# Half-array matmuls issued in turn over two PSUM banks in a two-block transformer kernel

## Chip, cores and metric

The kernel runs on one core of one Trainium2 chip. The metric is the device time of one execution in microseconds (us). Engines: PE (TensorE, matrix products), DVE (VectorE), ACT (ScalarE), POOL (GpSimd) and SP (SyncE, which issues most transfers). PE writes its products to PSUM, eight banks of [128, 512] floats.

## What is computed

256 tokens of width 2048 go through two blocks, each of two layers. The first block is attention: in layer 0 a sparse attention with compressed, selected and window branches, a differential attention with heads of 64 channels, and an attention over a memory; in layer 1 an attention to the 64 keys that an index score picks, and the memory again. The second block has in each layer four mixers beside each other (retention, hgrn2, mlstm, rwkv7, each 512 wide with heads of 64 channels) and a feed-forward part. The pieces with heads of 64 channels, cut from the reference:

```python
# differential attention: two score maps per head, 64 channels each
p = masked_softmax(jnp.einsum('bthcd,bshcd->bhcts', qb, k) * dq ** -0.5, key_pos[None, :] <= t[:, None])
a = p[:, :, 0] - lam * p[:, :, 1]
# index score of layer 1: 16 heads of 64 channels
rel = jax.nn.relu(jnp.einsum('bthd,bsd->bths', qi, k_idx))
score = jnp.einsum('bths,bth->bts', rel, wi)
# second block: each layer
mixed = jnp.concatenate([o_ret, o_hgrn, o_ml, o_rw], axis=-1) @ w_out[l]
h = h + rms_norm_2(mixed, norm_post_mix[l])
ffn = (jax.nn.silu(u @ w_ffn_gate[l]) * (u @ w_ffn_up[l])) @ w_ffn_down[l]
# rwkv7, per token and head of 64 channels
state = state * exp(logw) - (state kk) (a kk)^T + v k^T ;  y = state r
```

## The kernel before

All tokens stay on the chip; weights stream in pieces of [128, 1024] floats, which ACT (L205) and DVE (L206) split into two parts. Each product of a projection is three matmuls at L211 (`mm3`), which read and write the whole 128 by 128 array. In fp32, as in the mixers and attentions, one matmul of the program is two pairs of a weight load and a matmul in the trace, so a record count there is twice the program's count.

A *half-array* matmul uses 64 of the 128 rows (a product over the 64 channels of a head, operands in partitions 0 to 63 or 64 to 127) or 64 of the 128 columns (its result goes to 64 of the 128 partitions). The heads of even number lie in one half, those of odd number in the other. The sites, by the lines of the profile:

- differential attention, L451 in `soft`: per half (`c`) a bank with a mask product (L450, bf16) and a score per head in turn, then softmax on DVE and ACT. Other attentions call `soft` too, with scores over the full array.
- `pick`, L949: index scores; four (first token block) or two heads of one half per bank, then ACT's relu (L952) and one DVE instruction per head (L959).
- retention L1043 and L1044, mlstm L1235 and L1236: per head a bank, one score of 256 columns and one of 128, then DVE (mlstm L1237), then products over the full array. In mlstm the decays (L1228, L1230, exponential at L1233) of a head go first into a bank of their own.
- hgrn L1140: eight levels, per half a bank with two scores of 128 columns; L1144 (DVE) multiplies each bank with a mask. L1149 puts the results into 64 rows of bank 7 per half.
- rwkv: L1331 (low-rank inputs), L1409 and L1410 (`grams`: per source and half a bank with four products of 128 columns), L1446 and L1472 (products with the state S, in the second token block only, each followed by products over the full array into the same bank), L1481 and L1482 (update of S).

The helper `bank` takes the numbers of a use in turn; in the mixing phase rwkv has banks 3 and 4, the other mixers 5 and 6, results gathered over heads bank 7, projections 0 to 2. The final order on each engine isn't that of the code: a list scheduler of the build orders the instructions by their dependences, tiles and banks, and fills the gaps of a mixer with L211 of other projections. PE takes its instructions in that order.

Of the kernel before, what the change touches and what calls it, by code (L numbers as in the profile page):

```python
# [18 lines left out]
P = 128  # L19
T = 256  # L20
# [5 lines left out]
# ---------------------------------------------------------------- constants  # L26
# [11 lines left out]
class Slab:  # L38
    """Arrays of [128, n] packed side by side; at[name] is (offset, columns)."""
# [70 lines left out]
# ------------------------------------------------------------------ emitter  # L110
# tiles of each tag: of the whole run, of the first block, of the second block
# [4 lines left out]
# PSUM banks of each use: m projections, t their inputs' transposes, e what takes them on, x scores and transposes,  # L116
# o results gathered over heads, r rwkv
# [5 lines left out]
class Later:  # L123
    """Items that are computed where they are first asked for."""
# [10 lines left out]
def halves(x):  # L135
    """The two token blocks of a tile [128, 2, 512]."""
    return [x[:, m] for m in range(2)]


class Emitter:  # L140
# [34 lines left out]
    def on_the_way(self):  # L175
        """For what takes a projection out of PSUM, beside the attention of earlier ones."""
# [7 lines left out]
    def phase(self, **banks):  # L184
        """The numbers of the PSUM banks that each use takes in turn."""
# [12 lines left out]
    # -- weights: loaded in pieces of [128, j, n], split into two float32r parts  # L198
# [14 lines left out]
    def by_tokens(self, xg, w, c0, n):  # L213
        """x @ w[:, c0:c0+n] as two tiles [128 tokens, n]."""
# [12 lines left out]
    def by_channels(self, xg, w, c0, n):  # L227
        """(x @ w[:, c0:c0+n]).T as tiles [128 channels, 2, 256 tokens]."""
# [14 lines left out]
    def by_channels1(self, xg, w, c0, n):  # L243
        """(x @ w[:, c0:c0+n]).T, n < 128, as one tile [n, 256 tokens]."""
# [9 lines left out]
    def turned_back(self, xg, w, c0, n):  # L254
        """x @ w[:, c0:c0+n], n < 128, as two tiles [128 tokens, n]."""
# [7 lines left out]
    def group_block(self, yg, w, k0, cb):  # L263
        """y[:, k0:k0+512] @ w[k0:k0+512, cb*512:(cb+1)*512] per token block."""
# [9 lines left out]
    def out_group(self, yg, w, k0, dst, first):  # L274
        """dst[g][m] += y[:, k0:k0+512] @ w[k0:k0+512]."""
# [8 lines left out]
    # -- float32r pairs  # L284
# [3 lines left out]
    def split(self, dst, src, scale=None):  # L288
        """dst (hi, lo) = src * scale, hi rounded, lo the rest; src in PSUM or SBUF."""
# [9 lines left out]
    def transposes(self, out, srcs):  # L299
        """out[:, i] = srcs[i].T for blocks srcs[i]; out in PSUM."""  # L300
# [39 lines left out]
    def x_part(self, xg, kt, rows=slice(None)):  # L340
        """Rows of the kt-th channel block of a group list of pairs; the next group is made ahead."""
# [5 lines left out]
    def row_scale_of(self, X):  # L347
        """row_scale of X, computed when it is first needed."""
# [11 lines left out]
    def rsqrt(self, out, v, tmp, by=None):  # L360
        """out = by * v ** -0.5: a first guess from the exponent, three Newton steps; v becomes -v / 2."""
# [26 lines left out]
    def spread_rows(self, r):  # L388
        """[128, 256] with r[t] in every partition; r: [128 tokens, 2]."""
# [10 lines left out]
    def head_scale(self, src, nh, dh, rows=None, m=0, n=P, eps=EPS):  # L400
        """Per row and head r * rsqrt(mean((r * src)**2) + eps); src [n, nh*dh] in PSUM."""
# [9 lines left out]
    def gain_tables(self, tag, gain, cos, sin, dh, into=None):  # L411
        """cos * gain and sin * (gain with halves swapped), for rope of (x * gain)."""
# [1347 lines left out]
```

## Time and profile before

| | us |
|---|---|
| three timed runs: median (lowest, highest) | 3990.16 (3976.85, 3991.68) |
| span of the profiled execution | 3999.7 |
| PE busy | 3919.7 (98%) |
| DVE busy | 2377.9 (59%) |
| ACT busy | 1817.2 (45%) |
| mean granted TensorE clock | 0.972 |

The span runs from the first to the last instruction of the one profiled execution; the profile gives no other time of it, and its span lies 9.5 us above the median of the timed runs. The busy time of PE counts overlapping records once, and the end of a matmul record is modelled, so what a matmul costs is read from the start of one record to the start of the next.

### The profile page before, as it was taken

The numbers are of one execution on the slowest core, as the hardware profiler recorded it, in microseconds if no ns is written. First come the engines' busy times: TensorE is split into PE (matmuls) and PEld (weight loads), VectorE is DVE, ScalarE is ACT, GpSimd is POOL, SyncE is SP. The second block draws the span as 40 slices with busy tenths as digits, with TensorE's granted clock in tenths as the row PEclk, the third lists the DMA queues.
The fourth block names the chain that finished last, engine by engine and source line by source line (L and its number), as shares of the span: only waits on it lengthen the run. The fifth ranks groups of instructions, "written<-read, shape, count | busy, mean of one in ns | idle before, by whom it ended". The sixth has DMA issues, their size and how long they took to land.

```text
span 3999.7 us, 54714 instructions
## 1 busy us (share of the span) xinstructions
PE 3919.7 (98%) x21408; PEld 3282.1 (82%) x21408; DVE 2377.9 (59%) x4126; ACT 1817.2 (45%) x2463; POOL 0.2 (0%) x4
## 2 busy tenths in 40 slices
PE   9999999999999999999999999999999999999998
PEld 7878777788898988978888888898988978888886
DVE  6666667666664556574555556664566564555556
ACT  5545455454444355354344444534454354444443
POOL 0000000000000000000000000000000000000000
PEclk9999999999997899999999999996999999999999
DMA  7664545555632244556666666521344566666665
GB/s 237 194 174 121 168 135 146 169 168 163 196 92 59 85 127 140 171 180 184 189 185 185 185 188 187 156 81 54 94 142 143 169 190 185 185 188 184 185 187 165
DMA packets 402644, 633.64 MB, mean 158 GB/s; under 512 B 28081, under 2 KB 164017, under 8 KB 402385
## 3 DMA queue, kind: packets, MB, share of 16 engines
q1 hardware_dynamic: 399744, 624.70, 52.1%
q10 hardware_dynamic: 2640, 5.44, 0.4%
q8 instruction: 168, 2.75, 0.3%
q14 instruction: 92, 0.75, 0.1%
HBM read 623.77 MB, written 6.29 MB: 158 GB/s over the span
## 4 chain that ended last, share of the span: by engine, by line
PE 88%; DVE 6%; DMA 3%; ACT 2%; issue 1%; SPq 0%; ACTq 0%; DVEq 0%
PE b L211 73%; PE b L303 3%; DVE wlo L206 2%; PE b L1432 1%; PE b L1427 1%; PE b L451 1%; PE b L1149 1%; ACT whi L205 1%; PE b L478 1%; PE b L1140 1%; DMA wraw<-in_even_w_in_dram 0%; PE b L1409 0%; DMA wraw<-in_nsa_cmp_w_dram 0%; DMA wraw<-in_w_ffn_down_dram 0%; PE b L1230 0%
## 5 line engine op out<-in xcount | busy, mean ns | idle before, releaser
L206 DVE TENSOR_TENSOR wlo<-wraw,whi 128x1024 fp32r<-128x1024 f32 x1144 | 1393.7, 1219 | 1136.4 <-ACT whi L205 1134.4
L205 ACT CAST whi<-wraw 128x1024 fp32r<-128x1024 f32 x1144 | 1196.1, 1046 | 1567.6 <-PE b L211 1441.0
L211 PE MATMUL b<-whi,xt 128*128 128x512 f32 (+1 forms) x5888 | 1698.7, 371 | 0.0
L211 PEld LDWEIGHTS b<-whi,xt 128*128 128x128 f32 x5888 | 1062.8, 190 | 197.1 <-issue 3.7
L211 PE MATMUL b<-wlo,xt 128*128 128x512 f32 (+1 forms) x2944 | 1088.8, 370 | 3.5 <-DVE wlo L206 3.4
L211 PE MATMUL b<-whi,yt 128*128 128x512 f32 x2304 | 746.1, 400 | 1.5 <-ACT yt L293 1.5
L211 PEld LDWEIGHTS b<-wlo,xt 128*128 128x128 f32 x2944 | 559.8, 190 | 100.8 <-DVE wlo L206 7.3
L211 PE MATMUL b<-xt,whi 128*128 128x256 f32 (+3 forms) x2688 | 520.7, 291 | 2.3 <-ACT xt L296 2.0
L211 PEld LDWEIGHTS b<-whi,yt 128*128 128x128 f32 x2304 | 433.9, 189 | 108.2 <-issue 2.7
L211 PE MATMUL b<-wlo,yt 128*128 128x512 f32 x1152 | 461.8, 401 | 0.0
L211 PEld LDWEIGHTS b<-xt,whi 128*128 128x128 f32 (+3 forms) x2688 | 423.1, 191 | 14.3 <-ACT xt L296 3.3
L211 PE MATMUL b<-xt,wlo 128*128 128x256 f32 (+3 forms) x1344 | 388.9, 289 | 0.0
L211 PEld LDWEIGHTS b<-wlo,yt 128*128 128x128 f32 x1152 | 217.5, 189 | 52.4 <-issue 2.1
L211 PEld LDWEIGHTS b<-xt,wlo 128*128 128x128 f32 (+3 forms) x1344 | 256.6, 191 | 3.5 <-issue 1.5
L211 PE MATMUL b<-whi,g 128*128 128x512 f32 (+1 forms) x384 | 108.0, 360 | 0.4 <-ACT g L293 0.4
L282 DVE TENSOR_TENSOR r<-b,r 128x512 f32<-128x512 f32 x144 | 92.3, 683 | 0.0
L211 PEld LDWEIGHTS b<-whi,g 128*128 128x128 f32 (+1 forms) x384 | 61.7, 162 | 14.3 <-ACT g L293 0.9
L303 PE MATMUL b<-gains,X 128*128 128x128 f32 x232 | 39.0, 305 | 33.1 <-DVE small L370 15.6
L211 PE MATMUL b<-wlo,g 128*128 128x512 f32 (+1 forms) x192 | 68.7, 358 | 0.3 <-DVE wlo L206 0.2
L282 DVE TENSOR_TENSOR X<-b,X 128x512 f32<-128x512 f32 x96 | 63.0, 684 | 8.9 <-PE b L211 8.7
L1437 ACT COPY r<-b 128x512 f32<-128x512 f32 x40 | 23.4, 584 | 92.3 <-PE b L303 92.2
L303 PEld LDWEIGHTS b<-gains,X 128*128 128x128 f32 x232 | 30.5, 157 | 39.8 <-issue 25.9
(481 smaller groups left out, 3036.8 us busy)
## 6 DMA issues: line engine op xcount, KB each, us to landing
wraw<-in_w_in_dram SPq DMA_DIRECT2D x248, 512.0 KB, 3.7
wraw<-in_w_ffn_gate_dram SPq DMA_DIRECT2D x176, 512.0 KB, 3.7
wraw<-in_w_ffn_up_dram SPq DMA_DIRECT2D x176, 512.0 KB, 3.7
wraw<-in_w_ffn_down_dram SPq DMA_DIRECT2D x176, 512.0 KB, 3.7
wraw<-in_w_out_dram SPq DMA_DIRECT2D x128, 512.0 KB, 3.7
wraw<-in_even_w_in_dram SPq DMA_DIRECT2D x104, 512.0 KB, 3.6
wraw<-in_odd_w_in_dram SPq DMA_DIRECT2D x96, 512.0 KB, 3.6
wraw<-in_mem_w_kv_dram SPq DMA_DIRECT2D x32, 512.0 KB, 4.1
```

The lines of the kernel that those rows point to most:

```text
L205: nc.scalar.copy(hi, raw)
L206: nc.vector.tensor_sub(lo, raw, hi.bitcast(FT))
L211: self.nc.tensor.matmul(out, l[x], r[y], start=start and i == 0, stop=stop and i == 2, **kw)
L282: self.nc.vector.tensor_add(dst[cb][m], ps[m], dst[cb][m])
L303: self.nc.tensor.transpose(o, s, self.c("ident")[:n, :n])
L451: nc.tensor.matmul(ps[:, o : o + nk], l, r, start=not masks, stop=True, skip_group_check=True)
L478: self.nc.tensor.matmul(out, tt[:, i, j], vs[j], start=j == 0, stop=j == k - 1)
L1140: nc.tensor.matmul(ps[:, i], ek[r, i], eq[r, i], start=True, stop=True)
L1149: nc.tensor.matmul(out, vc[:, i * P + 64 * par : i * P + 64 * par + 64], am[:, par, i], start=False, stop=h == 1, skip_group_check=True)
L1427: mm(ps[:, i].rearrange("p (b k) -> p b k", k=h), gb[0][:, i], left(inv[:, i]), start=True, stop=True)
L1432: mm(ps[:, i], it[:, i], pl[:, i], start=True, stop=True)
L1437: nc.scalar.copy(it, b)
```

## The change

Where the halves were written one after the other, they are now written in turn: first of one half, first of the other, second of the one, and so on, into two banks that are both taken ahead. `soft` becomes `scores` (all masks first, then the scores of all sets in turn) and `exps`. In mlstm the decays of two heads come before the scores of both, and the sums for the denominator move from the decays' bank to the scores'. In rwkv the products with S of all heads come before the products that add to them. The state's update takes heads 0, 2, 1, 3. No arithmetic is added or removed. Comment lines, which the change also drops, are left out.

```diff
+    def scores(self, sets, nk):
+        nc = self.nc
+        res = [self.bank()[:, : len(items) * nk] for items in sets]
+        for ps, items in zip(res, sets):
+            for i, (_, _, masks) in enumerate(items):
+                for x, (ml, mr, mc) in enumerate(masks):
+                    o = i * nk + mc
+                    nc.tensor.matmul(ps[:, o : o + mr.shape[1]], ml, mr, start=x == 0 and i == 0, stop=False,
+                                     skip_group_check=True)
+        for i in range(len(sets[0])):
+            for ps, items in zip(res, sets):
+                l, r, masks = items[i]
+                nc.tensor.matmul(ps[:, i * nk : i * nk + nk], l, r, start=not masks and i == 0, stop=True,
+                                 skip_group_check=True)
+        return res
...
+    def pair_scores(self, qT, kT, i):
+        res = [self.bank() for _ in range(2)]
+        for ss, ts, c in ((slice(0, P), slice(0, T), slice(0, T)), (slice(P, T), slice(P, T), slice(T, 384))):
+            for par in range(2):
+                r = slice(64 * par, 64 * par + 64)
+                self.nc.tensor.matmul(res[par][:, c], kT[r, i, ss], qT[r, i, ts], start=True, stop=True)
+        return res
...
@@ hgrn
+            for i in range(2):
+                for par in range(2):
+                    r = slice(64 * par, 64 * par + 64)
+                    nc.tensor.matmul(pss[par][:, i], ek[r, i], eq[r, i], start=True, stop=True)
             for par in range(2):
-                r = slice(64 * par, 64 * par + 64)
-                ps = self.bank()[:, :T].rearrange("p (a t) -> p a t", a=2)
-                for i in range(2):
-                    nc.tensor.matmul(ps[:, i], ek[r, i], eq[r, i], start=True, stop=True)
...
@@ mlstm
+        for h in range(4):
+            if h % 2 == 0:
+                dms = [decays(h + x) for x in range(2)]
+                pss = self.pair_scores(qT, kT, h // 2)
+            dm, ps = dms[h % 2], pss[h % 2]
             nc.vector.scalar_tensor_tensor(dm, ps[:, :384], 0.125, dm, OP.mult, OP.mult)
...
-            db = pd[:, 384:386]
+            db = ps[:, 384:386]
...
@@ rwkv_half, grams
+                pss = [self.bank().rearrange("p (a x t) -> p a x t", a=2, x=2) for _ in range(2)]
+                for i in range(2):
+                    for x, by in enumerate((kk, r)):
+                        for par in range(2):
+                            q = heads[2 * par + i][2]
+                            mm(pss[par][:, i, x], src[q, i, t], by[q, i, t], start=True, stop=True)
...
@@ rwkv_half, products with the state
+            def of_state(src):
+
+                res = [self.bank()[:, :P].rearrange("p (i c) -> p i c", i=2) for _ in range(2)]
+                if S is not None:
+                    for i in range(2):
+                        for par in range(2):
+                            q = heads[2 * par + i][2]
+                            mm(res[par][:, i], src[q, i, t], S[q, i], start=i == 0, stop=False, skip_group_check=True)
+                return res
...
-                for h in range(4):
+                for h in (0, 2, 1, 3):
```

What the change does to the instructions' order, at three places of the first mixing phase. Names: `L211` is a projection's matmul, `b3` to `b7` are banks with the number of the tile behind them, `x2` means two program matmuls in a row.

PE, mlstm, around the scores of the second head before (L1235, L1236; decays at L1228, L1230):

```order
L1235 MATMUL b6_11858<-g2_11440,g2_11573 128x256
L1236 MATMUL b6_11858<-g2_11440,g2_11573 128x128
L211 MATMUL b0_11940<-xt_9177,whi_11942 128x256
L303 MATMUL b3_10819<-gains_63,r2_10815 128x128 x4
L1228 LDWEIGHTS identb2_9137
L1228 MATMUL b5_11851<-laterb_9139,identb2_9137 128x128
L1228 LDWEIGHTS identb2_9137
L1228 MATMUL b5_11851<-laterb_9139,identb2_9137 128x128
L1230 MATMUL b5_11851<-mx_11305,gains_63 128x384
```

and now around the scores of the second pair of heads (L1077 is `pair_scores`, L1251 and L1253 are the decays, L1457 and L1462 belong to rwkv):

```order
L1251 LDWEIGHTS identb2_9137
L1251 MATMUL b6_11876<-laterb_9139,identb2_9137 128x128
L1251 LDWEIGHTS identb2_9137
L1251 MATMUL b6_11876<-laterb_9139,identb2_9137 128x128
L1253 MATMUL b6_11876<-mx_11305,gains_63 128x384
L1462 MATMUL b4_10851<-r1_10849,r2_10815 128x64 x4
L1077 MATMUL b5_11883<-g2_11440,g2_11573 128x256
L1077 MATMUL b6_11884<-g2_11440,g2_11573 128x256
L303 MATMUL b3_10857<-gains_63,r2_10816 128x128 x4
L1457 MATMUL b4_10863<-r2_10816,r2_10783 128x64 x4
L1077 MATMUL b5_11883<-g2_11440,g2_11573 128x128
L1077 MATMUL b6_11884<-g2_11440,g2_11573 128x128
```

The scores of a head stood alone ahead of the next head's decays; now the decays of a second head stand ahead of both heads' scores, which alternate between banks 5 and 6.

PE, rwkv, first of the `grams`, before:

```order
L1409 MATMUL b3_10018<-r2_9692,r2_9690 128x128
L1410 MATMUL b3_10018<-r2_9688,r2_9690 128x128
L1409 MATMUL b3_10018<-r2_9692,r2_9690 128x128
L1410 MATMUL b3_10018<-r2_9688,r2_9690 128x128
L1409 MATMUL b4_10025<-r2_9692,r2_9690 128x128
L1410 MATMUL b4_10025<-r2_9688,r2_9690 128x128
L1409 MATMUL b4_10025<-r2_9692,r2_9690 128x128
L1410 MATMUL b4_10025<-r2_9688,r2_9690 128x128
```

and now:

```order
L1438 MATMUL b3_10018<-r2_9692,r2_9690 128x128
L1438 MATMUL b3_10018<-r2_9688,r2_9690 128x128
L1438 MATMUL b3_10018<-r2_9692,r2_9690 128x128
L1438 MATMUL b3_10018<-r2_9688,r2_9690 128x128
L1438 MATMUL b4_10019<-r2_9692,r2_9690 128x128
L1438 MATMUL b4_10019<-r2_9688,r2_9690 128x128
L1438 MATMUL b4_10019<-r2_9692,r2_9690 128x128
L1438 MATMUL b4_10019<-r2_9688,r2_9690 128x128
```

The code alternates, but the scheduler still sets all four products of one bank ahead of the four of the other, here and in all 16 of these sets.

PE, rwkv, second token block, products with the state (L1446, now L1476) and those that add to them (L1447, now L1486), before:

```order
L1446 MATMUL b4_10379<-st_10204,r2_9692 128x64
L1447 MATMUL b4_10379<-r2_10002,r2_10257 128x64
L1446 MATMUL b4_10379<-st_10204,r2_9692 128x64
L1447 MATMUL b4_10379<-r2_10002,r2_10257 128x64
L211 MATMUL b0_11450<-xt_9297,wlo_11543 128x256
L211 MATMUL b0_11450<-xt_9297,whi_11542 128x256
L1446 MATMUL b3_10385<-st_10204,r2_9692 128x64
L1447 MATMUL b3_10385<-r2_10002,r2_10257 128x64
L1446 MATMUL b3_10385<-st_10204,r2_9692 128x64
L1447 MATMUL b3_10385<-r2_10002,r2_10257 128x64
```

and now:

```order
L1476 MATMUL b4_10379<-st_10204,r2_9692 128x64 x2
L1486 MATMUL b4_10379<-r2_10002,r2_10257 128x64 x2
L211 MATMUL b0_11450<-xt_9297,wlo_11543 128x256
L211 MATMUL b0_11450<-xt_9297,whi_11542 128x256
L1476 MATMUL b3_10380<-st_10204,r2_9692 128x64 x2
L1486 MATMUL b3_10380<-r2_10002,r2_10257 128x64 x2
```

The two halves still stand apart, with two L211 between; within a half the two products with S now stand together. In the other places: hgrn's scores alternate in all 32 levels, its L1149 (now L1173) stood as four in a row or as two, two transposes (L303), two, and now as one, one transpose, three; retention's order stands as it was; `pick` alternates, with two to four L211 between its sets.

## Rows read from the trace of the kernel before

**Rows 1.** The page: busy time of the engines, chain of waits by engine

```profile
PE 3919.7 (98%) x21408; PEld 3282.1 (82%) x21408; DVE 2377.9 (59%) x4126; ACT 1817.2 (45%) x2463; POOL 0.2 (0%) x4
...
PE 88%; DVE 6%; DMA 3%; ACT 2%; issue 1%; SPq 0%; ACTq 0%; DVEq 0%
```

**Rows 2.** Windows, length, busy PE PEld DVE ACT POOL (instructions), granted clock, DMA share, GB/s

```profile
1080.00:1760.00 680.00, 660.00 (x4600) 590.58 (x4600) 394.96 (x784) 302.62 (x440) 0.00 (x0) 0.93 0.41 122
495.40:502.20 6.80, 6.80 (x19) 5.05 (x19) 1.61 (x7) 3.04 (x9) 0.00 (x0) 0.50 0.26 80
669.00:684.00 15.00, 14.11 (x83) 10.15 (x82) 14.19 (x40) 8.55 (x14) 0.00 (x0) 1.00 0.24 70
```

**Rows 3.** Timeline of PE (start, us, instruction, records xcount): scores of hgrn

```profile
1467.02 0.72 PE L1140 MATMUL b<-g 64*128 64x128 f32 x8
1467.67 0.50 PE L211 MATMUL b<-wlo,yt 128*128 128x512 f32 x1
```

**Rows 4.** Timeline of PE: one half of `grams` alone

```profile
1164.97 0.49 PE L1409 MATMUL b<-r,r 64*128 64x128 f32 x2
...
1166.06 0.39 PE L211 MATMUL b<-xt,whi 128*128 128x256 f32 x1
```

**Rows 5.** Timeline of PE: both halves of `grams`, four products and four

```profile
1125.89 0.49 PE L1409 MATMUL b<-r,r 64*128 64x128 f32 x2
...
1127.72 0.38 PE L211 MATMUL b<-xt,whi 128*128 128x256 f32 x1
```

**Rows 6.** Timeline of PE: retention, scores of two heads in turn

```profile
1632.20 0.71 PE L1043 MATMUL b<-g,g 64*128 64x256 f32 x4
...
1633.06 0.39 PE L211 MATMUL b<-whi,xt 128*128 128x256 f32 x1
```

**Rows 7.** Timeline of PE: products with the state, one half

```profile
1360.79 0.43 PE L1446 MATMUL b<-st,X 64*128 64x64 f32 x2
...
1361.88 0.43 PE L1447 MATMUL b<-r,r 128*128 128x64 f32 x2
1362.12 0.36 PE L211 MATMUL b<-wlo,xt 128*128 128x256 f32 x1
```

**Rows 8.** Timeline of PE: mlstm, a whole head, a divided one

```profile
1389.36 0.70 PE L1235 MATMUL b<-g,g 64*128 64x256 f32 x2
...
1390.20 0.39 PE L211 MATMUL b<-xt,whi 128*128 128x256 f32 x1
...
1392.46 0.70 PE L1235 MATMUL b<-g,g 64*128 64x256 f32 x2
1393.09 0.28 PE L1228 MATMUL b<-laterb,identb 128*128 128x128 bf16 x2
...
1394.14 0.48 PE L1236 MATMUL b<-g,g 64*128 64x128 f32 x2
1394.56 0.39 PE L211 MATMUL b<-xt,whi 128*128 128x256 f32 x1
```

**Rows 9.** Timeline of PE: differential attention, first token block, masks and scores

```profile
491.91 0.23 PE L450 MATMUL b<-futureb,identb 128*128 128x128 bf16 x1
...
497.26 0.79 PE L211 MATMUL b<-whi,xt 128*128 128x512 f32 x1
```

**Rows 10.** Timeline of PE: results of hgrn, two in a row and four

```profile
1463.19 0.65 PE L1149 MATMUL b<-g,a 128*64 128x128 f32 x4
...
1463.77 0.44 PE L303 MATMUL b<-gains,a 128*128 128x128 f32 x2
...
1469.03 0.83 PE L1149 MATMUL b<-g,a 128*64 128x128 f32 x8
1469.80 0.44 PE L303 MATMUL b<-gains,a 128*128 128x128 f32 x2
```

**Rows 11.** Groups by line (busy us, mean ns, idle before, releaser): mlstm, split weights

```profile
L206 DVE TENSOR_TENSOR wlo<-wraw,whi 128x1024 fp32r<-128x1024 f32 x1136 | 1390.2, 1224 | 1128.5 <-ACT whi L205 1126.5 <-issue 0.5
...
L1237 DVE SCALAR_TENSOR_TENSOR a<-b,a 128x384 f32<-128x384 f32 x16 | 8.9, 555 | 14.0 <-ACT a L1233 10.5 <-PE b L1236 3.5
```

More of the change, by code (lines that the diff above doesn't have):

```diff
@@ L440, in soft, with exps @@
     def soft(self, items, nk, fs):
+        return self.exps(self.scores([items], nk)[0], nk, fs)
+    def scores(self, sets, nk):
         nc = self.nc
-        n = len(items)
-        ps = self.bank()[:, : n * nk]
-        for i, (l, r, masks) in enumerate(items):
-            o = i * nk
-            for x, (ml, mr, mc) in enumerate(masks):
-                w = mr.shape[1]
-                nc.tensor.matmul(ps[:, o + mc : o + mc + w], ml, mr, start=x == 0, stop=False, skip_group_check=True)
-            nc.tensor.matmul(ps[:, o : o + nk], l, r, start=not masks, stop=True, skip_group_check=True)
+        res = [self.bank()[:, : len(items) * nk] for items in sets]
[11 more added lines that the diff above has]
+        return res
+    def exps(self, ps, nk, fs):
+        nc = self.nc
+        n = ps.shape[1] // nk
         ps3 = ps.rearrange("p (h k) -> p h k", h=n)
@@ L830, in diff @@
                 pts, cfs = [], []
+                both = (slice(0, 64), slice(64, 128))
+                scores = self.scores([[(qT[r, h, t], kT[r, h, :nk], self.causal(m)) for h in range(h0, h0 + step)]
+                                      for r in both], nk)
                 for c in range(2):
-                    r = slice(c * 64, c * 64 + 64)
-                    pt, sm = self.soft([(qT[r, h, t], kT[r, h, :nk], self.causal(m)) for h in range(h0, h0 + step)],
-                                       nk, fs[m].rearrange("p (h c) -> p c h", c=2)[:, c, h0 : h0 + step])
+                    pt, sm = self.exps(scores[c], nk, fs[m].rearrange("p (h c) -> p c h", c=2)[:, c, h0 : h0 + step])
                     pts.append(pt)
@@ L943, in pick @@
         for h0 in range(0, 16, 2 * step):
-            for par in range(2):
-                b = slice(64 * par, 64 * par + 64)
-                ps = self.bank()
-                for i in range(step):
-                    h = h0 + par + 2 * i
-                    nc.tensor.matmul(ps[:, i * nk : i * nk + nk], qi[h // 8][b, h % 8 // 2, m * P : m * P + P],
-                                     kiT[b, :nk], start=True, stop=True)
+            pss = [self.bank() for _ in range(2)]
+            for i in range(step):
+                for par in range(2):
+                    b = slice(64 * par, 64 * par + 64)
+                    h = h0 + par + 2 * i
+                    nc.tensor.matmul(pss[par][:, i * nk : i * nk + nk], qi[h // 8][b, h % 8 // 2, m * P : m * P + P],
+                                     kiT[b, :nk], start=True, stop=True)
+            for par in range(2):
                 rel = self.t([P, 512], "soft")
-                nc.scalar.activation(rel, ps, AF.Relu)
+                nc.scalar.activation(rel, pss[par], AF.Relu)
                 for i in range(step):
@@ L1036, in retention @@
         for h in range(4):
-            r = slice(64 * (h % 2), 64 * (h % 2) + 64)
             if h % 2 == 0:
@@ L1041, in retention @@
                 nc.sync.dma_start(dec, self.a["decay"][:, h0 * T : h0 * T + 2 * T].rearrange("p (h t) -> p h t", h=2))
[L1042 to L1044 removed]
+            if h % 2 == 0:
+                pss = self.pair_scores(qT, kT, h // 2)
+            ps = pss[h % 2]
             a = self.t([P, 384], "a3")
@@ L1465, in rwkv_half @@
             y = self.t([P, T], "r1").rearrange("p (i j c) -> p i j c", i=2, j=2)
+            pss = of_state(r)
             for par in range(2):
-                ps = self.bank()[:, :P].rearrange("p (i c) -> p i c", i=2)
                 for i in range(2):
                     h = 2 * par + i
-                    _, _, q, c = heads[h]
-                    if S is not None:
-                        mm(ps[:, i], r[q, i, t], S[q, i], start=True, stop=False)
-                    mm(ps[:, i], gk[1][:, h], vt[:, m, c : c + 64], start=S is None, stop=False)
-                    mm(ps[:, i], gb[1][:, h], nu[:, h], start=False, stop=True)
-                nc.scalar.copy(y[:, :, par], ps)
+                    c = heads[h][3]
+                    mm(pss[par][:, i], gk[1][:, h], vt[:, m, c : c + 64], start=S is None, stop=False,
+                       skip_group_check=True)
+                    mm(pss[par][:, i], gb[1][:, h], nu[:, h], start=False, stop=True, skip_group_check=True)
+                nc.scalar.copy(y[:, :, par], pss[par])
             if m == 0:
                 ps = self.bank()[:, :P].rearrange("p (i c) -> p i c", i=2)
-                for h in range(4):
+                for h in (0, 2, 1, 3):
                     _, i, q, c = heads[h]
```

49 lines of the change are left out of this document (22 added, 27 removed).

## Prediction

> **What bounds the kernel now.** I read the page first: the busy times, then the chain of work that ended last. TensorE is busy 98% of the span and holds 88% of the chain; DVE has 6%, transfers 3%, ACT 2% [rows 1]. So a saved microsecond of TensorE counts nearly in full, as long as what it waits for is ready. Next the windows: in the first mixing phase (the second, of the other layer, is built alike) TensorE works 660 of 680 us, and its granted clock averages 0.93 [rows 2]. The two levels being 0.5 (1.2 GHz) and 1 (2.4 GHz), that makes (1 − 0.93) × 2 × 680 = 95 us at half clock, which cost 48 us. The half-array matmuls lie in these two phases, in the differential attention, a part of which runs at half clock (0.50), and in `pick`, where DVE is busy 14.19 of 15.0 us [rows 2]. The rest, projections and feed-forward, is untouched.
>
> Then the timeline of TensorE, place by place; every price here is the distance from the start of one record to the start of the next. The question for each place is whether the halves overlap already.
>
> **They overlap where the second half stands close.** hgrn's scores have two program matmuls of one half and then two of the other, not alternated, yet the eight records take 1467.67 − 1467.02 = 0.65 us [rows 3], while eight records of one half alone take 1166.06 − 1164.97 = 1.09 [rows 4]. With four and four (`grams`) the overlap begins late: 16 records take 1127.72 − 1125.89 = 1.83, against 2.18 for two halves apart [rows 5]. So alternating gains nothing in groups of two, and something in groups of four; but there the scheduler undoes it (all 16 sets keep four and four). **hgrn scores 0, grams 0, retention 0** (its order stands; two of its heads in turn cost 1633.06 − 1632.20 = 0.86 [rows 6], the price of a pair below).
>
> The Trainium skill, "TensorE: Matmul & The Clock Gate", Part 3, The mechanism, states that matmuls run strictly in their program order and only weight loads are pulled ahead. By that, two halves issued one behind the other would not overlap; rows 3 against rows 4 speak against it, and what it would give is a rival below.
>
> **The price of changing between half and whole array.** In a half of the products with the state, the last two records take 1362.12 − 1361.88 = 0.24 before a whole-array matmul; all eight take 1.33, so the three changes inside cost (1.33 − 4 × 0.24) / 3 = 0.12 each [rows 7].
>
> **mlstm.** Before, each layer has eight heads. One stands among the L1331, in whose other half it is hidden; I count it 0, and the L1331 the same in both kernels. Three stand whole at 1390.20 − 1389.36 = 0.84; four are divided by decays or by rwkv, 0.63 + 0.42 = 1.05 [rows 8]. Sum 2.52 + 4.20 = 6.7. After, by the order, of four pairs one alternates in one piece and one stands half directly behind half, which overlaps as in rows 3, 0.86 each [rows 6]; one alternates but is divided, 0.65 for its scores of 256 columns and 0.42 for the others; one has two L211 between its halves, 2 × 0.84 = 1.7. That is 0.86 + 0.86 + 1.07 + 1.70 = 4.5. Two layers save 2 × 2.2 = 4.5 (unrounded). There are five fewer visits to half mode per layer, whose first change lies outside these distances: 10 × 0.12 = 1.2. **5.7**, bounds 3.5 (no changes saved, one more pair divided) and 6.5 (some of it at half clock).
>
> **Products with the state.** Two changes fewer in each of 16 halves, 0.24 to 0.28 with the rounding of the records: 16 × 0.25 = **4.0**, bounds 3 and 4.5. The halves themselves stay apart.
>
> **Differential attention.** In the first token block eight masks and eight scores stood in turn, 497.26 − 491.91 = 5.35 us, the end at half clock [rows 9]. Now eight masks (0.12 each, a record of the 0.24 above: 1.0) and eight scores, 16 records, in alternation (2 × 0.65): 2.3. Saves 3.1. Were a mask 0.23, its whole record, it would be 2.2. The second block's sets stay apart and only gather their masks: four sets with two changes fewer, 1.0. **4.1**, bounds 2.9 and 4.6. The masks of the other attentions, 35 places where a mask stood between scores, all on the whole array: 0 to 2, I take **1**.
>
> **hgrn's results** (L1149). Two of a half alone cost 1463.77 − 1463.19 = 0.58, four in a row 1469.80 − 1469.03 = 0.77 [rows 10]. Before, 18 of 32 levels were two, transposes, two (1.16) and 14 four. Now 28 are one, transpose, three: 0.24 + 0.12 for the one, 0.58 or more for the three, 0.94. So 18 × 0.22 = 4.0 gained, and 10 to 14 lose 0.17, 2.0: **2.0**, bounds −2 (the three don't overlap at all) and 4.
>
> **`pick`**: under a busy DVE, 0 to 3, I take **1**. **The state's update**, four clusters that alternate sooner: **0.5**, 0 to 1.
>
> Sum 5.7 + 4.0 + 4.1 + 1 + 2.0 + 1 + 0.5 = **18.3** us; by the bounds 7 to 26. Nothing is added to DVE, ACT or the queues. What is costed at nothing is the cover: while DVE and ACT work on scores, TensorE is filled with L211 of other projections. The profiled execution's span is 9.5 us above the median of the timed runs; the 18 us are taken from the span's rows and subtracted from the median, 3990.2 − 18 = **3972**.
>
> **Rivals.**
>
> 1. *The saved time turns into waits.* mlstm now needs two heads' decays before the first score is used, and its DVE step waited for ACT's exponential, 10.5 us idle over 16 heads against 3.5 for its scores [rows 11]; the state's results feed a chain of DVE and ACT, and `pick` is DVE's [rows 2]. If TensorE stands idle there as long as it was spared, 5.7 + 4.0 + 1 go: −8, **3982**. For it: those rows. Against: TensorE idles only 20 of the 680 us, L211 lie between.
>
> 2. *The clock gives more.* The half clock costs 48 us in the first mixing phase; mixers of which TensorE does the same in less time, with fewer changes, might be spared a third of it, 16 us: −34, **3956**. For it: the diff's half-clock stretch lies right where its masks and scores alternated [rows 2, 9]. Against: no row ties the half clock of the mixing phase to the half-array matmuls. The reverse, 16 lost, is −2, inside the range.
>
> 3. *Slower: a use now takes both of its banks at once.* Where before one bank was evacuated while the other was filled, TensorE can now stand before a pair until both are free. 27 sites take pairs that way (8 in mlstm, 8 with the state, 6 in `pick`, 5 in differential attention). What stands ahead of an evacuation on DVE is at most a weight split, 1.22 us, then the evacuation, 0.56 [rows 11]: 1.78 each. All 27 cost 48: +30, **4020**. It decides the sign from 11 sites on (11 × 1.78 = 19.6) and passes 20 us of loss from 22 on. Against it: the build's order has L211 ahead of most of these sites, which need other banks.
>
> The Trainium skill, "TensorEngine Tiling (Array Packing)", Restrictions and Gotchas, Gotcha 1: PSUM Pressure, warns of this: row tiles have to write to different banks, so they press on PSUM more. No row of the kernel before shows such a wait at these sites.
>
> 4. *The halves do not overlap yet unless alternated.* Then hgrn's 32 levels gain too, 32 × (1.09 − 0.65) = 14: −32, **3958**. Rows 3 already show the 0.65.
>
> 5. *The alternation does nothing*; only changes of mode are saved: mlstm 1.2, state 4.0, diff 3.5: −9, **3981**. Rows 6 speak against it.
>
> **How the numbers follow.** Forecast 3972 (its own range 3964 to 3983): 0.50. Rivals: waits 0.18, clock 0.18, banks 0.07, halves 0.03, no effect 0.04. A measurement of this kernel can tell about 0.5%, 20 us, from no change. The forecast lies just inside that bound, so 0.22 of its 0.50 is faster and 0.28 the same. Faster: 0.22 + 0.18 + 0.03 = 0.43; same: 0.28 + 0.18 + 0.04 = 0.50; slower: 0.07. The range holds the forecast, the waits and the clock with the spread of the timed runs (15 us): 3948 to 3994.
>
> **What the profile after would show.** L1077: alternated pairs at 0.86 from first record to the next L211, not 2 × 0.84. L1438 (`grams`) still 1.09 for a half and 1.6 to 1.8 for two; L1163 (hgrn scores) still 0.65. L1476: four records in a row, halves near 1.1. L1173: one and three, 0.94 together. In the differential attention the masks and scores of the first block in some 2.3 us. The granted clock of the mixing phases 0.93 for the forecast, 0.95 for rival 2. The group L1237 and the waits of TensorE at L1251 and L1476 tell rivals 1 and 3: idle time of TensorE in the first mixing phase near 20 us for the forecast, near 25 for rival 1 (half of its 10 us), near 34 for rival 3 (half of its 16 sites in the mixers, 14 us). I am wrong if the time is outside 3964 to 3983 although these prices hold: then something that none of the rows shows, such as the place of the L211, moves more than the small matmuls do.

## The result

| | before | after |
|---|---|---|
| median of 4 runs, us (lowest, highest) | 3983.84 (3976.85, 3991.68) | 3939.39 (3937.86, 3948.32) |
| span of the profiled execution, us | 3999.7 | 3937.6 |
| mean granted clock of that execution | 0.972 | 0.982 |

The ratio is 0.9891, 95% interval 0.9871 to 0.9911: 44 us faster. The forecast was 3972 and its range 3948 to 3994, so the time lies below the range. Of the 33 us between forecast and time, 6 are the base: the forecast was taken from the median of three runs, 3990, and four have 3984. The changed kernel gained what the prediction's list of savings says, a little more, and about as much again from the granted clock, which the prediction had left as it was.

Each run comes with its span and its mean granted clock, and these two split the time. I call **loss** the span times (1 − clock): a stretch at half clock, 1.2 GHz in place of 2.4, counts with half its length. The **rest**, span times clock, is what the execution would take at full clock throughout. The clock is given to three digits, which leaves ±2 us of a single run's rest open. Over all later runs of the kernel before, in five sets of 17 to 29, the means of the rest are 3891.6 to 3892.6 us and those of the loss 92 to 95. Within a set the rest lies within 8 to 10 us (standard deviation 2 to 3), the loss within 37 to 57: nearly all the scatter of the kernel before (3950 to 4012 us) is the clock. One execution of the kernel before (4759 us) and one of an experiment (kk product alone, 6369 us) ran at a far lower clock, 0.736 and 0.617, and are left out of every mean. The changed kernel's four runs have a rest of 3867.5 and a loss of 71.9. So **the rest fell by some 25 us and the loss by some 22**.

### The profile page after: what moved, and what is told of

The parts are those of the page before. It is cut to its first block, busy times and chain, and to the rows that moved or that the text cites. A ratio compares the mean times of both kernels' runs of the same rounds, so it can differ in the third digit from the quotient of the medians.

```text
span 3937.6 us, 54729 instructions
## 1 busy us (share of the span) xinstructions
PE 3864.2 (98%) x21408; PEld 3235.9 (82%) x21408; DVE 2379.0 (60%) x4126; ACT 1806.0 (46%) x2455; POOL 0.2 (0%) x4
## 4 chain that ended last, share of the span: by engine, by line
PE 79%; DVE 5%; ACT 2%; DMA 1%; issue 1%; DVEq 0%; SPq 0%; ACTq 0%
PE b L211 67%; PE b L303 3%; DVE wlo L206 1%; PE b L1462 1%; PE b L1457 1%; PE b L1438 1%; PE b L1173 1%; ACT whi L205 1%; PE b L1077 1%; PE b L1163 1%; PE b L457 0%; PE b L491 0%; PE b L1253 0%; DMA g<-in_decay_dram 0%; PE b L1001 0%
## 5 line engine op out<-in xcount | busy, mean ns | idle before, releaser
L211 PE MATMUL b<-whi,xt 128*128 128x512 f32 (+1 forms) x5888 | 1688.0, 369 | 0.1
L211 PEld LDWEIGHTS b<-whi,xt 128*128 128x128 f32 x5888 | 1054.2, 188 | 194.6 <-issue 3.9
L211 PE MATMUL b<-wlo,xt 128*128 128x512 f32 (+1 forms) x2944 | 1083.8, 368 | 2.5 <-DVE wlo L206 2.3
L211 PE MATMUL b<-whi,yt 128*128 128x512 f32 x2304 | 742.3, 400 | 1.5 <-ACT yt L293 1.5
L211 PEld LDWEIGHTS b<-wlo,xt 128*128 128x128 f32 x2944 | 555.2, 189 | 99.7 <-DVE wlo L206 5.7
L211 PEld LDWEIGHTS b<-whi,yt 128*128 128x128 f32 x2304 | 433.8, 189 | 105.8 <-ACT yt L293 2.0
L211 PE MATMUL b<-xt,whi 128*128 128x256 f32 (+3 forms) x2688 | 509.7, 287 | 2.3 <-ACT xt L296 2.0
L211 PE MATMUL b<-wlo,yt 128*128 128x512 f32 x1152 | 463.1, 402 | 0.0
L211 PEld LDWEIGHTS b<-xt,whi 128*128 128x128 f32 (+3 forms) x2688 | 416.2, 188 | 13.1 <-issue 3.9
L211 PE MATMUL b<-xt,wlo 128*128 128x256 f32 (+3 forms) x1344 | 386.1, 287 | 0.0
L211 PEld LDWEIGHTS b<-wlo,yt 128*128 128x128 f32 x1152 | 218.5, 190 | 51.6 <-issue 1.4
L211 PEld LDWEIGHTS b<-xt,wlo 128*128 128x128 f32 (+3 forms) x1344 | 252.5, 188 | 4.3 <-issue 1.8
L211 PE MATMUL b<-whi,g 128*128 128x512 f32 (+1 forms) x384 | 107.8, 360 | 0.4 <-ACT g L293 0.4
L211 PEld LDWEIGHTS b<-whi,g 128*128 128x128 f32 (+1 forms) x384 | 61.7, 162 | 14.3 <-ACT g L293 0.9
L303 PE MATMUL b<-gains,X 128*128 128x128 f32 x232 | 38.4, 303 | 32.8 <-DVE small L370 16.6
L211 PE MATMUL b<-wlo,g 128*128 128x512 f32 (+1 forms) x192 | 68.7, 358 | 0.0
L1467 ACT COPY r<-b 128x512 f32<-128x512 f32 x40 | 23.4, 584 | 93.7 <-PE b L303 93.7
L303 PEld LDWEIGHTS b<-gains,X 128*128 128x128 f32 x232 | 29.9, 156 | 40.8 <-issue 27.6
```

The lines of the kernel that those rows point to most:

```text
L211: self.nc.tensor.matmul(out, l[x], r[y], start=start and i == 0, stop=stop and i == 2, **kw)
L303: self.nc.tensor.transpose(o, s, self.c("ident")[:n, :n])
L1467: nc.scalar.copy(it, b)
```

## The profile after

The page: busy times, and the chain that ended last.

```profile
PE 3864.2 (98%) x21408; PEld 3235.9 (82%) x21408; DVE 2379.0 (60%) x4126; ACT 1806.0 (46%) x2455; POOL 0.2 (0%) x4
...
PE 79%; DVE 5%; ACT 2%; DMA 1%; issue 1%; DVEq 0%; SPq 0%; ACTq 0%
```

TensorE is still the bound, with the same number of records as in [rows 1]; it is busy 55 us less (its share of the clock's gain is contained in that), DVE as long as before.

Timeline of TensorE, places of the prediction (start, length, instruction, records).

```profile
488.30 0.62 PE L452 MATMUL b<-futureb,identb 128*128 128x128 bf16 x8
488.85 1.16 PE L457 MATMUL b<-g,g 64*128 64x128 f32 x16
489.94 0.50 PE L211 MATMUL b<-whi,xt 128*128 128x512 f32 x1
...
1116.34 1.90 PE L1438 MATMUL b<-r,r 64*128 64x128 f32 x16
1118.17 0.39 PE L211 MATMUL b<-xt,whi 128*128 128x256 f32 x1
...
1190.71 0.66 PE L1476 MATMUL b<-st,r 64*128 64x64 f32 x4
1191.30 0.66 PE L1486 MATMUL b<-r,r 128*128 128x64 f32 x4
1191.77 0.36 PE L211 MATMUL b<-xt,wlo 128*128 128x256 f32 x1
...
1354.69 0.93 PE L1077 MATMUL b<-g,g 64*128 64x256 f32 x8
1355.55 0.39 PE L211 MATMUL b<-xt,wlo 128*128 128x256 f32 x1
...
1423.27 0.71 PE L1163 MATMUL b<-g 64*128 64x128 f32 x8
1423.91 0.73 PE L211 MATMUL b<-whi,yt 128*128 128x512 f32 x2
1424.57 0.79 PE L1173 MATMUL b<-g,a 128*64 128x128 f32 x8
...
1429.30 0.43 PE L1173 MATMUL b<-g,a 128*64 128x128 f32 x2
1429.66 0.33 PE L303 MATMUL b<-gains,a 128*128 128x128 f32 x1
1429.92 0.65 PE L1173 MATMUL b<-g,a 128*64 128x128 f32 x6
1430.50 0.33 PE L303 MATMUL b<-gains,a 128*128 128x128 f32 x1
```

Read from start to start: masks and scores of the differential attention 489.94 − 488.30 = 1.64 us, against 5.35 [rows 9]; a set of grams still 1.83 [rows 5]; a half of the products with the state 1191.77 − 1190.71 = 1.06 against 1.33 [rows 7]; an mlstm pair 0.86, against 0.84 for one head [rows 8]; hgrn's scores 0.64 as before [rows 3]; its results 0.36 and 0.58 [rows 10]. These are the prices that the prediction had worked out, or lower.

The clock, by windows (window, length, busy PE PEld DVE ACT POOL, granted clock, DMA share, GB/s). Of the changed kernel, the two mixing phases, then the stretch from the split of weight piece 352 to that of 368 in the first:

```profile
1080.00:1760.00 680.00, 662.61 (x4679) 589.16 (x4679) 412.34 (x822) 315.11 (x469) 0.00 (x0) 0.95 0.41 128
2560.00:3240.00 680.00, 663.67 (x4601) 585.90 (x4600) 410.90 (x817) 311.49 (x461) 0.00 (x0) 0.95 0.41 128
1168.80:1295.50 126.70, 124.52 (x910) 114.80 (x909) 69.83 (x175) 53.33 (x85) 0.00 (x0) 0.89 0.23 72
```

Of the kernel before, the second mixing phase (the first is in [rows 2]) and the stretch between the same two weight pieces:

```profile
2560.00:3240.00 680.00, 662.25 (x4629) 590.42 (x4628) 400.67 (x797) 306.80 (x453) 0.00 (x0) 0.93 0.41 121
1180.60:1337.40 156.80, 153.45 (x943) 139.86 (x941) 73.96 (x184) 57.56 (x91) 0.00 (x0) 0.76 0.20 58
```

Between the same two pieces of work 156.8 us became 126.7. The loss in it went from 0.24 × 156.8 = 37.6 to 0.11 × 126.7 = 13.9, which is 24 of the 30 us; TensorE's idle time was 3 us and is 2. The records in between are not quite the same (943 and 910), so a part of the other 6 us is work that moved elsewhere. It is the stretch in which rwkv first multiplies with the state (from 1202 before, from 1190 now) and mlstm starts. A single profile's clock is one draw of many, so the verdicts below go by the means over all runs of a kernel.

## The experiments

Rest and loss are given as the mean over a kernel's runs minus that of the runs of before taken beside them, with 95% intervals. There were 12 runs of most kernels, 5 to 12 of all.

| kernel | rest | loss | ratio (interval) |
|---|---|---|---|
| attentions and pick alone | −6.7 ± 1.6 | +4.9 ± 5.7 | 0.9991 (0.9976 to 1.0007) |
| mlstm alone | −6.2 ± 1.9 | +4.5 ± 6.1 | 0.9991 (0.9975 to 1.0008) |
| hgrn alone | −6.2 ± 1.4 | −1.6 ± 7.4 | 0.9981 (0.9960 to 1.0003) |
| rwkv's low-rank inputs alone | +0.4 ± 1.9 | +4.3 ± 8.4 | 1.0012 (0.9989 to 1.0035) |
| rwkv alone | −4.4 ± 1.8 | −20.1 ± 8.6 | 0.9940 (0.9921 to 0.9960) |
| products with the state and update alone | −5.4 ± 3.5 | −25.9 ± 10.0 | 0.9918 (0.9893 to 0.9944) |
| both products, no update | −3.6 ± 4.4 | −24.2 ± 11.7 | 0.9923 (0.9893 to 0.9952) |
| kk product alone | −2.3 ± 1.8 | −5.8 ± 10.6 | 0.9982 (0.9954 to 1.0010) |
| r product alone | −2.8 ± 2.0 | −5.7 ± 7.2 | 0.9965 (0.9950 to 0.9980) |
| update alone | −1.0 ± 1.4 | −0.6 ± 8.1 | 0.9989 (0.9972 to 1.0007) |
| all mixers, attentions and pick as before | −17.3 ± 2.0 | −16.7 ± 6.4 | 0.9916 (0.9894 to 0.9938) |
| all but rwkv | −18.2 ± 1.9 | +3.9 ± 5.2 | 0.9970 (0.9953 to 0.9987) |
| all but products with the state and update | −18.0 ± 2.3 | +9.3 ± 7.0 | 0.9976 (0.9956 to 0.9996) |
| all but the low-rank inputs | −21.7 ± 2.6 | −27.1 ± 10.2 | 0.9879 (0.9846 to 0.9912) |
| products and update, first product of each half three times | −0.4 ± 1.6 | −7.3 ± 7.1 | 0.9976 (0.9955 to 0.9997) |
| all but the low-rank inputs, third bank for rwkv | +6.5 ± 1.2 | −13.9 ± 5.9 | 0.9982 (0.9963 to 1.0000) |

**1. Does the clock answer to the order or to the moment?** Four kernels split the change into attentions and mixers, and rwkv and the other mixers. Edit of the first: `scores` and `exps` in the attentions, pairs of banks in `pick`, and nothing else; in both mixing phases TensorE's rows are those of before.

```diff
+            pss = [self.bank() for _ in range(2)]
+            for i in range(step):
+                for par in range(2):
```

> The kernel before with the change in the differential and the other attentions and in pick alone; the order of TensorE in both mixing phases is word for word that of before. Measured in the profiles of before and after up to the first mixing phase: 11.8 us gained, 8.4 of work and 3.4 of clock. Theory A (the clock is given back by what TensorE does in the mixers): 12 us faster, ratio 0.997, half clock in the two mixing phases as in the kernel before within 15 us of the 190. Theory B (where the half clock falls depends on when a phase begins, not on its order): the phases begin 12 us earlier, so their half clock changes by 20 us or more, up or down, and the time is 0 to 30 us lower.

The rest fell by 6.7 and the loss did not fall. An earlier start of the mixing phases does not give clock back, which speaks against theory B.

All mixers, with attentions and `pick` as before:

> The kernel before with the change in all mixers, attentions and pick as before. Theory A: the mixers' 16 us of work and about 34 us of clock as in the profile after, less what the timed runs of before have less of it: 30 to 50 us faster, ratio 0.988 to 0.992, half clock in the mixing phases near 130 us. Theory B: 16 us faster by work, the clock anywhere; ratio 0.990 to 0.998.

The rest fell by 17.3, the loss by 16.7: 33 us, as theory A has it.

rwkv alone (the hunks of `rwkv_half`: low-rank inputs, grams, products with the state, update), and the changed kernel with exactly these taken back:

> The kernel before with the change in rwkv alone (low-rank inputs, grams, products with the state, update). By the rows of after its work saves 16 x 0.3 for the products with the state, 2.2 for the update, nothing for the grams, 7 us in all. Theory A with rwkv as the place (the half clock lies where rwkv runs): 20 to 35 us faster. Theory A with mlstm as the place: 7 us faster, ratio 0.998. Theory B: 7 us and a clock change of either sign.

> The changed kernel with rwkv as before. Theory A with rwkv as the place: 17 to 22 us faster than before, ratio 0.995. Theory A with mlstm as the place: 35 to 40 us faster, ratio 0.991. Theory B: 20 us of work, the clock anywhere.

rwkv alone gives 20 us of loss back, with only 4 of the rest. Everything else gives 18 of the rest and no loss. The place is rwkv.

**2. Which part of rwkv, and do the others hold what they promised?** The grams have no run of their own: the trace of rwkv alone, which contains them, differs in TensorE's order from that of the products and the update alone only around the low-rank inputs, in as many places (64) as the low-rank inputs alone move.

> The kernel before with rwkv's low-rank inputs alone alternated (four matmuls at L1331 per set; the build then also sets the projections' matmuls around rwkv's first token block otherwise). rwkv's whole change gave back 20 us of clock loss (span times one minus the granted clock, mean over the runs) and 4 us of the rest. Theory L (the order of the fillers that this moves): some 15 to 20 us of clock, under 1 us of the rest. Theory T (products with the state): no change of either, within 4 us.

> The kernel before with rwkv's products with the state gathered and the update of the state in turn, low-rank inputs as before. Theory T: 15 to 20 us of clock, 4 us of the rest. Theory L: 4 us of the rest alone. Should both give part of it, the clock answers to how often the array changes between half and whole, whichever site it is.

The low-rank inputs move the fillers in rwkv's first block, but neither rest nor loss. The products with the state and the update bring 26 us of loss. Windows of the two mixing phases in the profile of that kernel:

```profile
1080.00:1760.00 680.00, 662.21 (x4678) 588.19 (x4677) 408.69 (x820) 311.93 (x466) 0.00 (x0) 0.95 0.43 126
2560.00:3240.00 680.00, 662.88 (x4667) 586.70 (x4666) 413.40 (x824) 316.77 (x471) 0.00 (x0) 0.97 0.44 128
```

0.95 and 0.97 where before had 0.93 in both; TensorE is busy as long.

> The kernel before with mlstm alone changed. The changed kernel with rwkv as before lost 98 us to the clock, as the kernel before (94), so no clock gain is expected by either theory; of the rest (mean of span times granted clock), 5.7 us by the prediction's sum; if mlstm's freed time goes into waits, 0 to 2.

> The kernel before with hgrn alone changed. Prediction: 2.0 us of the rest, by the records 29.3 in place of 32.0 us for its results and 0.2 for its scores, 2.9; no clock. If the order of the fillers alone moves the clock, 10 us or more of it in either direction.

mlstm brought 6.2 of the rest, as worked out; it put nothing into waits. hgrn brought 6.2 where 2 to 3 were expected. Neither moved the loss beyond its interval.

**3. Products or update, changes or fillers?** The two products with the state apart, and the update apart. The edit of the second (the first is the same with `kk` and `u`), and of the third:

```diff
+            pss = of_state(r)
...
-                    if S is not None:
-                        mm(ps[:, i], r[q, i, t], S[q, i], start=True, stop=False)
```

```diff
-                for h in range(4):
+                for h in (0, 2, 1, 3):
```

> The kernel before with the first of the two products with the state (kk S, L1446) gathered, two and two in each half, nothing else. On TensorE only these eight halves change; the projections' matmuls that fill the gaps stay where they stood. The three changes (products with kk, products with r, update) gave back 26 us of clock together. Theory S (changing between half and whole array lowers the clock): 5 to 13 us of clock. Theory F (the gain lies in the order of the fillers and of mlstm around them, which the products with r move): no clock. Rest: 8 x 0.25 = 2 us by both.

> The kernel before with the second product with the state (r S, L1472) gathered ahead of the products that add to it, nothing else. Here the build also sets projections' matmuls, the low-rank inputs and mlstm's decays around it otherwise. Theory F: 20 to 26 us of clock. Theory S: 5 to 13. Theory U (the update): none. Rest: 8 x 0.25 = 2 us.

> The kernel before with the update of the state in the order of heads 0, 2, 1, 3, nothing else moves. Rest: the four clusters took 4.9 us before and 2.7 in the changed kernel, 2 us. Theory U: 20 us of clock or more. Theories F and S: none.

The rest came near what was expected, 2.3, 2.8 and 1.0 for 2 each. The gain in loss of the two products is near 6 each, inside the intervals; the update has none. Neither theory F (20 us or more with the fillers that the r product moves) nor theory U holds.

Then both products without the update, and a kernel that keeps these, the update too, but issues the first product of each half three times:

> The kernel before with both products with the state gathered (kk S and r S), the update as before. Each of the two alone gave back 6 us of clock (loss 92 to 86.5), the update alone 1; the three together 26. Theory of shares (each adds its own): 12 us of clock, loss near 81. Theory of a threshold (the stretch of rwkv's small matmuls leaves half clock only once enough is taken out of it, and both products do that): 20 to 26, loss near 70. Rest: 4 to 5 us.

```diff
-                            mm(res[par][:, i], src[q, i, t], S[q, i], start=i == 0, stop=False, skip_group_check=True)
+                            for _ in range(3 if i == 0 else 1):
+                                mm(res[par][:, i], src[q, i, t], S[q, i], start=i == 0, stop=False, skip_group_check=True)
```

> rwkv's products with the state gathered and the update in turn, as in the kernel that lost 69 us to the clock, but the first of the two products of each half is issued three times (same result each time), so that 2 x 16 more half-array matmuls stand in the row, without any further change between half and whole array. Theory C (the changes set the clock): loss stays at 69, rest 16 x 0.44 = 7 us more. Theory H (the time spent on half the array at that place sets it): loss back to 85 or more.

Both products without the update: loss 70.6, 24 us lower. That is nearer to the threshold's 20 to 26 than to the sum of the shares, 12, but the shares' intervals are wide (5.8 ± 10.6 and 5.7 ± 7.2), so a threshold is possible and not shown. Compared with the r product alone, TensorE's order in this kernel differs at the kk products only, so the order of the fillers is the same in both; it does not give the gain by itself. With more half-array products at the same place the loss went from 69 back to 88 (19 ± 12) and the rest up by 5, where 7 was expected. That is as theory H has it: at these sites no further change between half and whole array was added. But the fillers and some of mlstm's decays and scores stand elsewhere too, in over a hundred places of TensorE's order, so the repeated products are not shown to be the only cause. Whether the same time on the whole array would do it as well was not run. The mean clock of the kernels with both products and with the repeated ones, in their profiled executions:

```profile
core 0: 3961.0 us, clock 0.981
```

```profile
core 0: 3973.6 us, clock 0.980
```

By one execution each the two could not be told apart; the means over 6 and 12 runs, 0.982 and 0.978, do it.

**4. In the changed kernel.**

> The changed kernel with rwkv's products with the state and the update of the state as before, all other parts changed. If those two sites carry the clock in the changed kernel too: loss 95 us or more in place of the changed kernel's 72, rest 5 to 6 us above its 3867.5, so some 30 us slower than the changed kernel. If the clock there comes from the changes together: loss 72 to 85.

Without the two sites the loss is 102, against 72 with them, and the rest is 6 us higher. The kernel is 38 us slower than the changed one, and the mixing phases stand at before's clock:

```profile
1080.00:1760.00 680.00, 661.43 (x4610) 588.66 (x4609) 405.99 (x816) 309.53 (x462) 0.00 (x0) 0.93 0.42 123
2560.00:3240.00 680.00, 663.42 (x4579) 589.36 (x4578) 404.10 (x815) 309.31 (x461) 0.00 (x0) 0.93 0.41 121
```

So the clock gain of the changed kernel needs the products with the state (the update alone gave none); all other parts together do not give it.

> The changed kernel with rwkv's low-rank inputs as before. Alone they were worth 0 of the rest and -4 of clock. If that carries over: 0 to 4 us faster than the changed kernel, 45 to 50 below before.

3940.2 us, the changed kernel's 3939.4 within its scatter. The low-rank inputs are worth nothing there either.

A third bank for rwkv, on top of that:

```diff
-BANKS_MIX = dict(m=(0, 1, 2), t=(3, 4), r=(3, 4), x=(5, 6), o=(7,))
+BANKS_MIX = dict(m=(0, 1), t=(3, 4), r=(2, 3, 4), x=(5, 6), o=(7,))
```

> The same, with rwkv given a third bank (2, 3, 4) and the projections of the mixing phases left with two (0, 1). In the changed kernel all 16 sets of grams stood four and four, since the second bank was not free; here every other set alternates. If a set in turn costs 1.1 in place of 1.8 us: 8 x 0.7 = 6 us of the rest gained. If the projections wait for their bank: 10 us or more lost in TensorE's idle time.

Every other set was expected to alternate. In the trace 4 of the 16 do: the starts of their 16 records span 0.89 us, where the same sets took 1.63 or more without the third bank and the other sets take 1.6 or more. So a second bank that isn't free had kept these four together; for the others that is not shown. And the kernel takes 3981 us, the rest 28 us more than without the third bank. Its first mixing phase, and, over the whole execution, TensorE's waits for two instructions of DVE (line, waited for: us, times, longest):

```profile
1080.00:1760.00 680.00, 650.22 (x4633) 575.05 (x4632) 406.35 (x817) 310.73 (x463) 0.00 (x0) 0.96 0.42 124
```

```profile
PE b L303 <- DVE tok L437: 15.2, 13, 1.6
...
PE b L211 <- DVE etmp L433: 8.7, 8, 1.1
```

TensorE idles 30 us in this phase against 17 in the changed kernel, 4 of them at L211, which waits for what takes projections out of their two banks (L433).

## Why the prediction was wrong

**The sum of the work was right in kind and 7 us short.** Forecast 18.3 with bounds 7 to 26, measured 25. By parts, forecast against the rest of the experiment that does it alone: attentions and `pick` 6.1 against 6.7; mlstm 5.7 against 6.2; products with the state and update 4.5 against 5.4; hgrn 2.0 against 6.2. Alone they add up to 24.5, so the parts do not stand in each other's way. The mis-sized term is **hgrn's results**. The prices of its records were met, 0.36 and 0.58 for one and three [rows 10]; added over the trace, from record to record, its two sites shortened by 2.9 us, and the transposes beside them took 0.8 more, which together is about the forecast's 2.0. The other 4 us are the cover between scores and results, which the sum put at nothing. TensorE may start the results only when DVE has multiplied the scores with the mask (L1144). In the kernel before, 20 of the 32 levels had a single L211 in that gap, as here (starts of TensorE, DVE, and TensorE's weight load, with its wait in brackets):

```profile
1462.62 0.50 PE L211 MATMUL b<-whi,yt 128*128 128x512 f32 x1
1462.71 0.42 DVE L1144 TENSOR_TENSOR g<-b,consts 128x256 f32<-128x256 f32 x1 [1.33 <-PE b L1140]
1463.19 0.41 PEld L1149 LDWEIGHTS b<-g,a 128*64 128x64 f32 x4 [0.39 <-DVE g L1144]
```

The gap is 1463.19 − 1462.62 = 0.57, and DVE ends at 1463.13. In the changed kernel no gap has a single L211, and 20 have two, which take 1424.57 − 1423.91 = 0.66: one costs 0.33 there, so some 0.2 of the 0.57 had been waiting. The record of the waiting L211 is drawn nearly to the end of the gap, so little of it shows as idle time. Over hgrn's two stretches the L211 of this group add up to 4.3 us less with hgrn alone changed. That the gap was a wait for DVE is read from these rows; no run changes DVE's product alone.

Inside the attentions the parts were off, too. Masks and scores took 1.64 where 2.3 was worked out, as eight bf16 masks in a row take 488.85 − 488.30 = 0.55, 0.07 each and not 0.12; but of the 5.35 before, 0.9 was half clock [rows 2], which the prediction counted as work. `pick`, added from record to record, went from 11.4 to 8.6, where 1 was taken.

**What costs nothing cost nothing.** hgrn's scores, grams and low-rank inputs gave 0, as taken. Elsewhere the cover held: in the changed kernel TensorE idles 17 us of the first mixing phase (20 before). mlstm's DVE step does wait longer, but TensorE does not:

```profile
L1264 DVE SCALAR_TENSOR_TENSOR a<-b,a 128x384 f32<-128x384 f32 x16 | 8.4, 554 | 23.4 <-PE b L1077 23.4
```

Its idle time grew from 14.0 to 23.4 us, and the releaser changed: no longer ACT's exponential, which is now ahead, but the scores [rows 11]. Rival 1 (waits) and rival 3 (both banks at once) named places where waits could come; none of them shows.

**The step that failed is the clock.** The prediction kept the half clock of the mixing phases as it was, since no row tied it to the half-array matmuls, and gave the rival that a third of one phase's loss returns 0.18, at 16 us. 22 us returned, in both phases, whose clock rose to the 0.95 that the prediction had named as that rival's sign. Its own sign of being wrong came true: the prices held and the time lay outside; what moved more than the small matmuls do was the clock. A row on the place was to be had: the half clock in [rows 2] is not spread over the phase; 38 of its 48 us of loss lie in the one stretch shown above, 1180.6 to 1337.4, among the small matmuls of rwkv and mlstm. It would not have said which of them return it. The runs do: 4 to 5 us of work taken from rwkv's products with the state were worth 20 to 26 us of clock, while 18 us of work elsewhere were worth none. Standing at half clock does not decide it: in the profile before, 3.8 of 16.5 us of mlstm's scores, 3.1 of 4.9 of the update and 2.5 of 12.6 of the products with the state ran at half clock, and only the edit of the last returned any. Work and clock together are 25 + 22 = 47 us by the means, 44 by the medians; rival 2 with its own sizes (18 + 16) pointed to 3956. Why the clock answers at these sites, and whether there is a threshold, is not settled: the runs show where and how much.

**Alternation as such** was worth nothing at retention, hgrn's scores and the grams, for the two reasons of the prediction: groups of two overlap by themselves, and groups of four keep their order where a bank isn't free (shown for 4 of the 16 sets of grams). In mlstm, `pick` and the differential attention no run separates it from the gathering. The largest single effect came from an edit that doesn't alternate halves at all: the two halves of the products with the state still stand apart, but the products were gathered within a half.

## What to carry to other kernels

Split every run into span times clock and span times one minus clock before comparing kernels: the first scatters by 2 or 3 us here (standard deviation) and over a dozen runs shows a gain of 6 us that the times alone, with 15 us of scatter, cannot. When small matmuls are regrouped near a stretch at half clock, expect that the clock may return several times what was saved, and find out by a run: here one site did it, and others in the same stretch returned their own length alone. Look at the gaps between small matmuls, too: one filler in a gap in which another engine works left TensorE waiting, where two fitted. Alternating two halves gained nothing here where two matmuls of a half stood beside two of the other, or where the build kept four and four together.

## What the runs showed of the hardware

The loss of one kernel is not one number: identical runs of the kernel before had mean granted clocks from 0.970 to 0.987, with the rest within 11 us. The half clock came at much the same places of the program in the profiles, but not in every execution at each of them. Divide the stretch above at weight piece 364. Its second part (1274 to 1337 us in the kernel before) was at half clock for 27 to 41 us in all eight profiles of kernels in which neither product was gathered, and for 0 to 38 in those with both of them. Its first part, which holds the first products with the state, was at half clock for 10 to 34 us in the eight, for 0 to 8 in the seven with both, and for 20 in the one with repeated products. This is the first part before, in the changed kernel, and with repeated products:

```profile
1180.60:1274.40 93.80, 90.45 (x586) 83.09 (x585) 46.77 (x104) 43.84 (x64) 0.00 (x0) 0.82 0.26 74
1168.80:1239.40 70.60, 68.42 (x541) 62.88 (x539) 44.90 (x99) 39.90 (x61) 0.00 (x0) 1.00 0.32 99
1175.20:1254.50 79.30, 79.18 (x552) 72.86 (x550) 45.00 (x100) 38.47 (x58) 0.00 (x0) 0.87 0.30 86
```

Where it was at half clock, the same small matmuls took nearly twice as long: an mlstm head of 0.84 [rows 8] took 1363.27 − 1361.70 = 1.57 in the changed kernel, by this timeline:

```profile
1361.70 1.64 PE L1077 MATMUL b<-g,g 64*128 64x256 f32 x4
1363.27 0.58 PE L211 MATMUL b<-xt,whi 128*128 128x256 f32 x1
```

And half-array matmuls of two halves overlap without being alternated: 0.65 us for two and two before, 0.64 after. The Trainium skill ("TensorE: Matmul & The Clock Gate", Part 3, The mechanism) has matmuls run strictly in program order; these two numbers speak against that, since the order changed and the time did not, and the measurement decides.
